# Score products of two attention stages: from three half-array passes per head to two full-array passes

## The chip, the cores and the metric

The kernel runs on one core of one Trainium2 chip. The metric is device time in microseconds, the median of several runs of the whole program. TensorE (PE in the rows) multiplies, VectorE (DVE) and ScalarE (ACT) do the elementwise work, SyncE (SP), ScalarE and GpSimd (POOL) issue the DMAs.

## The reference

Two blocks run one after the other on 512 tokens of 1024 features, all in float32. The first block has two layers and also carries 256 context tokens. Each layer computes a modulated RMS norm, one wide input projection, a gated convolution, neighbourhood attention (NA: 8 heads, a bias per head), window attention (WA: 8 query heads over 2 key heads, a window of 128 tokens on either side, a sink) and a gated sum of the three. What matters here is the window attention:

```python
def window_attention(q, k, v, k_ctx, v_ctx, sink):
    ...
        s_w = jnp.einsum('bqkgd,bskd->bkgqs', q_n, k_n).astype(jnp.float32) * scale
        s_w = jnp.where(valid, s_w, -jnp.inf)
        s_c = jnp.einsum('bqkgd,bnkd->bkgqn', q_n, k_ctx).astype(jnp.float32) * scale
        p = sink_softmax(jnp.concatenate([s_w, s_c], axis=-1), sink_b).astype(v.dtype)
```

The second block is a gated linear recurrence, a convolutional feed-forward layer, a sparse attention and another feed-forward layer. The sparse attention has 16 query heads over 4 key heads of 64 features and three branches: compressed keys, selected blocks (at 512 tokens all eight blocks are chosen, so this is causal attention) and a window of 512 (causal too). Both of the last two compute, per head,

```python
        s = jnp.einsum('bgrqd,bgkd->bgrqk', qc, kw, preferred_element_type=f32)
        s = s - sl * dist_w.astype(f32)
        p = masked_softmax(s, m_w)
```

## The kernel before

Float32 products are made exact by splitting each operand into two float32r parts, a high and a low one, and summing three products: high by high, high by low, low by high. Almost all products are of this kind, with 128 rows of the array in use: `mm_t` (L140 to L142, moving tiles of 512 or 256 columns) and `mm_n` (L151 to L153, 256 columns).

An attention head has 64 features, so a head's queries and keys take 64 rows. Two heads of a pair lie on rows 0 to 63 and 64 to 127, each head's high and low queries in two column ranges of the same rows. `scores` (L489) issues, for each of the three combinations of parts, one matmul per head of the unit, on the two halves of the rows in turn. NA has its own form of it at L516. In the sparse attention `scores` (L1457) does the same for a pair of heads, a query block and a branch.

The keys of WA (`Kw`) and of the sparse branches (`KS`) already lie on both halves of the rows, since the heads of a pair share a key head.

Work in WA comes in units. Per layer, two groups `u` of four heads, two pairs in each; a pair has the units (query block 0, both heads), (1, head 0), (1, head 1), (2, head 0), (2, head 1), (3, both heads), and in layer 0 two more for the context's queries. A unit's scores go to PSUM banks of the tag "s" (four of them), its softmax is done by DVE and ACT, and three units later its probabilities are transposed (`att_tr`, L582 and L585) and, at the end of a pair, multiplied with the values (`pv`, L609 and L630). `weave` mixes other products in as fill: the queries of the next group, gates, the input of the convolution and, in the last group, single taps of the convolution on DVE (L911).

The queries of WA are made by `wa_q`: product, RMS norm per head, rotation on DVE, four transposes, and then `to_T_nat` (L477 to L482) writes both parts, high by ACT and low by DVE, in natural token order. The context's queries go through `to_T` (L462 to L468). The transposes of the last token group are held back in `pend` until a later product has been issued.

The sparse attention handles two heads `f` at a time: `queries` makes the product, scales it on DVE into `qf`, splits it into `Q` (`split`, L199 and L200), and writes the distance bias `M`. Units are (branch, query block) in the order of `KORD`; a unit is closed two units later (transposes L1518, and after a branch's last unit the product with the values, L1526). The queries of the next two heads are mixed in as fill, by a budget of 0.32 of the TensorE time that each unit reports.

Engines execute their own instructions in order. The order is fixed when the program is built, by a scheduler that takes the program's order as priority and may pull later work forward when its inputs and a buffer are there. `wh`, `wl` (four buffers each) and `wr` (two) hold weights and are shared with `Q`, and `M`.

Of the kernel before, what the change touches and what calls it, by code (L numbers as in the profile page):

```python
# [19 lines left out]
P = 128  # L20
# [24 lines left out]
PTQ = (0, 0, 1, 2)                  # first query block that meets a key block's band  # L45
PT0 = (0, 2, 5, 8)                  # where its probabilities start
# [8 lines left out]
def weave(main, fill, ratio):  # L55
    """both in step: for each unit of tensor engine time of main, ratio units of fill; then the rest of fill"""
# [12 lines left out]
class K:  # L69
    """Pools and the pieces that both blocks use."""  # L70
# [22 lines left out]
    # ---- PSUM tiles: one bank each  # L93
# [15 lines left out]
    # ---- weights: a part is loaded and split exactly into two float32r tiles  # L109
# [5 lines left out]
    def load_w(self, src, kt, m, prio=50):  # L115
        """src [128, kt * m] -> per k tile the pair of parts [128, m]"""
# [28 lines left out]
    # ---- out[token, feature] += act[k, token] W[k, feature]  # L145
# [10 lines left out]
    # ---- 1/sqrt(v) for a small tile, from the bits and three Newton steps  # L156
# [46 lines left out]
# x tokens in the first block: column by column, the last 8 columns first  # L203
# [3 lines left out]
def nat(n, b, g=None):  # L207
    """pairs of views with axes (column, row): of n [p, 512] in natural order
    and of b, in block order, whole or its half g"""
# [6 lines left out]
def first_block(k):  # L216
# [24 lines left out]
    # ---- modulation: part 0 (shift and scale, in two halves of the features) and part 1 (gate)  # L241
    MOD, GS, GATE = {}, {}, {}

    def mod_pieces(l, part, h, pool, tag, bufs, psum=k.s_):
        """a product of 1024 columns for both streams, as background pieces"""
# [45 lines left out]
    for l in range(2):  # L291
# [15 lines left out]
        with tc.tile_pool(reuse_waits="tile", name=f"nrm{l}", bufs=2) as np_:  # L307
# [55 lines left out]
            if l == 0:  # L363
                # keys and values of the first heads: the first half of the sum runs while
                # the second half of the modulation comes in
# [46 lines left out]
        with tc.tile_pool(reuse_waits="tile", name=f"att{l}", bufs=2) as ap:  # L412
# [79 lines left out]
            def att_qk(un):  # L492
# [36 lines left out]
                if nb:  # L529
                    scores(heads, sb, Q, qi, K_, ki, qb * P, un["band"][0] * P, nb)  # L530
# [1183 lines left out]
```

## Time and profile before

| What | Value |
|---|---|
| Median of 3 runs | 2909.45 us (2908.74 to 2911.26) |
| Span of the profiled execution | 2907.6 us |
| Difference of the two | 1.85 us |
| PE busy | 2847.9 us, 98% |
| DVE busy | 1950.6 us, 67% |
| ACT busy | 1116.1 us, 38% |
| WA of layer 0, layer 1 (first to last score product) | 328 to 478 us, 1177 to 1279 us |
| Sparse attention | 2244 to 2450 us |

The profiled execution's own time is its span, 2907.6 us, and 1.85 us lie around it when it is set beside the median. Matmuls overlap one another, and their ends are modelled, so what a matmul costs is read from the distance between the starts of two matmuls that follow each other and not from its duration. A row of the timeline merges neighbours of one kind: it gives the start of the first, the time to the end of the last, and their number.

### The profile page before, as it was taken

What the parts mean: (1) busy time and instruction counts of PE and PEld (TensorE: products, weight loads), DVE (VectorE), ACT (ScalarE), POOL (GpSimd) and SP (SyncE); (2) the same over time, 40 slices, a digit from 0 to 9 for tenths busy, and PEclk for the clock granted to TensorE, in tenths of its full rate; (3) what the DMA queues carried; (4) which work ended last, traced back from release to release, by engine and by line L of the source; (5) the groups of instructions that cost most, each with busy time, mean ns of one, the idle gap of its engine ahead of it and who ended that gap; (6) DMA issues with size and microseconds to landing.
All of it is one profiled execution on the core that took longest, in us unless ns stands there. A gap on an engine that the chain in (4) does not pass through costs nothing.

```text
span 2907.6 us, 41432 instructions
## 1 busy us (share of the span) xinstructions
PE 2847.9 (98%) x15812; PEld 2317.3 (80%) x15812; DVE 1950.6 (67%) x4673; ACT 1116.1 (38%) x2218; POOL 0.7 (0%) x6
## 2 busy tenths in 40 slices
PE   6999999999999999999999999999999999999998
PEld 4887877788887888778888878888888666888886
DVE  5667789994544667999757866636543777663663
ACT  4444453122322444542334743222333666322221
POOL 0000000000000000000000000000000000000000
PEclk9999999999999999999999999999999999999999
DMA  6111011531224221112233232232242001223322
GB/s 222 65 63 50 31 37 52 159 110 59 67 75 158 90 73 62 44 57 91 100 106 104 95 101 96 89 107 98 90 133 98 23 16 51 95 91 98 102 89 78
DMA packets 79542, 248.68 MB, mean 86 GB/s; under 512 B 8944, under 2 KB 16496, under 8 KB 79344
## 3 DMA queue, kind: packets, MB, share of 16 engines
q1 hardware_dynamic: 75888, 238.69, 25.4%
q10 hardware_dynamic: 3456, 7.34, 0.8%
q8 instruction: 125, 2.05, 0.3%
q14 instruction: 73, 0.60, 0.1%
HBM read 239.71 MB, written 4.19 MB: 84 GB/s over the span
## 4 chain that ended last, share of the span: by engine, by line
PE 88%; DVE 4%; ACT 1%; DMA 1%; issue 1%; DVEq 0%; ACTq 0%
PE g L140 22%; PE g L142 21%; PE g L141 21%; PE g L151 3%; PE g L153 2%; PE g L152 2%; PE s L489 2%; PE s L1457 2%; PE g L1526 1%; PE t L1518 1%; PE o L609 1%; PE t L585 1%; PE t L582 1%; PE s L516 1%; DMA wada<-in_w_ada_dram 1%
## 5 line engine op out<-in xcount | busy, mean ns | idle before, releaser
L126 ACT CAST wh<-wr 128x1024 fp32r<-128x1024 f32 (+2 forms) x392 | 392.6, 1002 | 834.1 <-PE g L141 592.9
L140 PE MATMUL g<-Hh,wh 128*128 128x512 f32 x1736 | 690.6, 398 | 0.5 <-DVE Yb L1253 0.4
L141 PE MATMUL g<-Hl,wh 128*128 128x512 f32 x1736 | 682.0, 393 | 0.0
L142 PE MATMUL g<-Hh,wl 128*128 128x512 f32 x1736 | 681.7, 393 | 0.0
L127 DVE TENSOR_TENSOR wl<-wr,wh 128x1024 fp32r<-128x1024 f32 (+2 forms) x392 | 454.9, 1161 | 313.4 <-ACT wh L126 312.6
L140 PEld LDWEIGHTS g<-Hh,wh 128*128 128x128 f32 x1736 | 326.3, 188 | 77.8 <-issue 7.4
L142 PEld LDWEIGHTS g<-Hh,wl 128*128 128x128 f32 x1736 | 325.7, 188 | 72.8 <-issue 4.2
L141 PEld LDWEIGHTS g<-Hl,wh 128*128 128x128 f32 x1736 | 326.4, 188 | 66.2 <-issue 3.2
L151 PE MATMUL g<-wh,Hh 128*128 128x256 f32 x640 | 187.2, 293 | 1.6 <-ACT Hh L359 1.3
L911 DVE SCALAR_TENSOR_TENSOR cv<-apad,cv 128x499 f32<-128x499 f32 (+22 forms) x305 | 187.2, 665 | 0.6
L153 PE MATMUL g<-wh,Hl 128*128 128x256 f32 x640 | 183.2, 287 | 0.0
L152 PE MATMUL g<-wl,Hh 128*128 128x256 f32 x640 | 182.8, 286 | 0.0
L140 PE MATMUL g<-fh,wh 128*128 128x512 f32 x384 | 149.4, 389 | 0.0
L141 PE MATMUL g<-fl,wh 128*128 128x512 f32 x384 | 149.4, 389 | 0.0
L142 PE MATMUL g<-fh,wl 128*128 128x512 f32 x384 | 149.4, 389 | 0.0
L151 PEld LDWEIGHTS g<-wh,Hh 128*128 128x128 f32 x640 | 123.0, 192 | 9.2 <-issue 5.2
L153 PEld LDWEIGHTS g<-wh,Hl 128*128 128x128 f32 x640 | 122.4, 192 | 5.5 <-issue 4.1
L152 PEld LDWEIGHTS g<-wl,Hh 128*128 128x128 f32 x640 | 122.8, 192 | 1.3 <-issue 0.8
L1274 DVE TENSOR_TENSOR fxp<-g,nb 128x512 f32<-128x512 f32 x48 | 33.2, 692 | 127.9 <-PE g L142 127.9
L553 ACT ACTIVATE pr<-s,m 128x512 f32<-128x512 f32 (+1 forms) x128 | 80.8, 634 | 82.6 <-DVE m L551 61.1
L1166 DVE TENSOR_TENSOR Xs<-Xs,g 128x512 f32<-128x512 f32 x48 | 33.0, 688 | 113.6 <-PE g L142 113.5
L140 PE MATMUL g<-Ch,wh 128*128 128x256 f32 x352 | 101.2, 287 | 0.0
(403 smaller groups left out, 5240.1 us busy)
## 6 DMA issues: line engine op xcount, KB each, us to landing
wr<-in_ffn_w_in_dram SPq DMA_DIRECT2D x96, 512.0 KB, 3.4
wr<-in_w_in_t_dram SPq DMA_DIRECT2D x88, 512.0 KB, 3.4
wada<-in_w_ada_dram SPq DMA_DIRECT2D x48, 512.0 KB, 4.5
wr<-in_ffn_w_out_dram SPq DMA_DIRECT2D x64, 384.0 KB, 3.1
wr<-in_w_in_n_dram SPq DMA_DIRECT2D x32, 512.0 KB, 3.6
wr<-in_lru_w_in_dram SPq DMA_DIRECT2D x20, 512.0 KB, 3.4
wr<-in_w_o_dram SPq DMA_DIRECT2D x16, 512.0 KB, 3.5
bt<-in_nab_dram SPq DMA_DIRECT2D x48, 128.0 KB, 2.4
```

The source lines that it names most:

```text
L126: nc.scalar.copy(h[:, :n], r[:, :n])
L127: nc.vector.tensor_sub(lo[:, :n], r[:, :n], h[:, :n].bitcast(F32))
L140: mm(o, a, hi(k), start=k == 0, stop=False)
L141: mm(o, a, lo(k), start=False, stop=False)
L142: mm(o, b, hi(k), start=False, stop=k == KT - 1)
L151: mm(o, h, w[k][0], start=k == 0, stop=False)
L152: mm(o, h, w[k][1], start=False, stop=False)
L153: mm(o, lo(k)[:, t0:t0 + P], w[k][0], start=False, stop=k == KT - 1)
L489: nc.tensor.matmul(dst[i], Q[sl, a, qi, q0:q0 + P], K_[sl, b, ki, k0:k0 + kn], start=a + b == 0, stop=a == 1)
L553: AC.activation(pr, un["S"][i][:, :nb + 256], AF.Exp, bias=m[:, 2:3], accum_out=m[:, 3:4])
L911: V.scalar_tensor_tensor(d, src, wc, d, op0=ALU.mult, op1=ALU.add)
L1457: nc.tensor.matmul(S_[i][:, :nn], Q[sls[i], x, qb * P:(qb + 1) * P], KS[b][sls[i], y, g, :nn], start=x + y == 0, stop=x == 1)
```

## The change

The queries of a head of WA or of a sparse branch are laid out anew: its high part on one half of the 128 rows and its low part on the other, in one column range. A matmul over all 128 rows with the keys' high part (which lie on both halves) then gives high by high plus low by high in one go, and a second one with the keys' low part gives the rest (and low by low, which was left out before). So three matmuls of 64 rows per head become two of 128 rows. In WA, units with 256 band keys also do band and context in one matmul of 512 columns instead of two of 256. NA keeps its three passes.

[...] In WA the DMAs (`swap`) are issued on GpSimd's queue, once for all 512 tokens of a group and once for the context's queries; the temporary is `btall`, which held NA's biases before and holds early convolution taps later. In the sparse attention they are issued on SP's queue, and the temporary is a buffer of the tag "wl". Lines that only lose a comment are left out.

```diff
+            def to_T2(raw, dst, g, gain, tmp):
+                t = k.t_()
...
+                tv = t.rearrange("p (a n) -> p a n", a=2)
+                d4 = dst.rearrange("p (a i) n -> p a i n", i=2)
+                x = tmp.rearrange("p (a n) -> p a n", a=2)
+                c = slice(g * 256, g * 256 + 256)
+                for lo, h, l_ in ((0, d4[0:64, :, 0, c], x[0:64]), (64, x[64:128], d4[64:128, :, 1, c])):
+                    sl = slice(lo, lo + 64)
+                    AC.activation(h, tv[sl], AF.Identity, scale=gain[sl])
+                    V.scalar_tensor_tensor(l_, tv[sl], gain[sl], h.bitcast(F32), op0=ALU.mult, op1=ALU.subtract)
+                swap(d4, x, c)
+
+            def swap(d4, x, c):
+                nc.gpsimd.dma_start(out=d4[64:128, :, 0, c].bitcast(F32), in_=x[0:64].bitcast(F32))
+                nc.gpsimd.dma_start(out=d4[0:64, :, 1, c].bitcast(F32), in_=x[64:128].bitcast(F32))
+
+            def to_T2_nat(raw, dst, g, tmp):
...
+                for pr in range(2):
+                    tv = t[:, pr * 256:(pr + 1) * 256]
+                    for i, hi, lo in ((0, dst[:, 2 * pr, 0:S], tmp[:, pr]), (1, tmp[:, pr], dst[:, 2 * pr + 1, 0:S])):
+                        sl = slice(64 * i, 64 * i + 64)
+                        for (h, b), (l_, _) in zip(nat(hi[sl], tv[sl], g), nat(lo[sl], tv[sl], g)):
+                            AC.copy(h, b)
+                            V.tensor_sub(l_, b, h.bitcast(F32))
+                if g == 1:
+                    swap(dst.rearrange("p (a i) n -> p a i n", i=2), tmp, slice(0, S))
...
-            def scores(heads, dst, Q, qi, K_, ki, q0, k0, kn):
+            def scores(na, heads, dst, Q, qi, K_, ki, q0, k0, kn):
+                if not na:
+                    for i in heads:
+                        for b in range(2):
+                            kk = K_[:, b, ki, k0[0]:k0[0] + kn]
+                            if len(k0) > 1:
+                                kk = bass.AP(tensor=kk.tensor, offset=kk.offset, ap=[list(kk.ap[0]), [k0[1] - k0[0], 2], [1, kn]])
+                            nc.tensor.matmul(dst[i], Q[:, 2 * qi + i, q0:q0 + P], kk, start=b == 0, stop=b == 1)
+                    return
                 for a, b in ((0, 0), (0, 1), (1, 0)):
...
-                scores(heads, sc_, Q, qi, K_, ki, qb * P, 512, 256)
-                if nb:
-                    scores(heads, sb, Q, qi, K_, ki, qb * P, un["band"][0] * P, nb)
-                return len(heads) * 3 * (256 + nb) / 2400
+                if nb == 256:
+                    two = lambda v: v.rearrange("p (s n) -> p s n", s=2)
+                    scores(na, heads, {i: two(S_[i]) for i in heads}, Q, qi, K_, ki, qb * P, (un["band"][0] * P, S), 256)
...
+                return len(heads) * (3 if na else 2) * (256 + nb) / 2400
...
             def wa_q(u):
-                QW[u] = slot("qw", F32R).rearrange("p (s a n) -> p s a n", s=2, a=2)
+                QW[u] = slot("qw", F32R).rearrange("p (h n) -> p h n", h=4)
+                tmp = btall.bitcast(F32R).rearrange("p (a n) -> p a n", a=2)
...
-                        pend.append(lambda r=rope(raw, rq, g, 4, 1), g=g: to_T_nat(r, QW[u], g))
+                        pend.append(lambda r=rope(raw, rq, g, 4, 1), g=g: to_T2_nat(r, QW[u], g, tmp))
                     else:
-                        pend.append(lambda r=raw: to_T(r, QW[u], 2, qg[:, 1:2]))
+                        pend.append(lambda r=raw: to_T2(r, QW[u], 2, qg[:, 1:2],
+                                                        ap.tile([P, 512], F32R, tag="raw", name=k.nm("qx"), bufs=NRAW)))
...
-                Q = k.wp.tile([P, WMAX], F32R, tag="wh", name=k.nm("nQ"), bufs=4).rearrange("p (a n) -> p a n", a=2)
+                Q = k.wp.tile([P, WMAX], F32R, tag="wh", name=k.nm("nQ"), bufs=4).rearrange("p (i n) -> p i n", i=2)
+                qx = k.wp.tile([P, WMAX], F32R, tag="wl", name=k.nm("qx"), bufs=4)[:, :S]
                 st["Q"] = Q
-                k.split(Q[:, 0], Q[:, 1], qf)
+                k.split(Q[0:64, 0], qx[0:64], qf[0:64])
+                k.split(qx[64:128], Q[64:128, 1], qf[64:128])
+                nc.sync.dma_start(out=Q[64:128, 0].bitcast(F32), in_=qx[0:64].bitcast(F32))
+                nc.sync.dma_start(out=Q[0:64, 1].bitcast(F32), in_=qx[64:128].bitcast(F32))
...
-                for x, y in ((0, 0), (0, 1), (1, 0)):
-                    for i in range(2):
-                        nc.tensor.matmul(S_[i][:, :nn], Q[sls[i], x, qb * P:(qb + 1) * P], KS[b][sls[i], y, g, :nn],
-                                         start=x + y == 0, stop=x == 1)
-                return 6 * nn / 2400
+                for i in range(2):
+                    for y in range(2):
+                        nc.tensor.matmul(S_[i][:, :nn], Q[:, i, qb * P:(qb + 1) * P], KS[b][:, y, g, :nn],
+                                         start=y == 0, stop=y == 1)
+                return 4 * nn / 2400
```

## Rows read from the trace of the kernel before

**Rows 1.** Page, parts 1 and 4: busy time; the chain that ended last, by engine.
```profile
PE 2847.9 (98%) x15812; PEld 2317.3 (80%) x15812; DVE 1950.6 (67%) x4673; ACT 1116.1 (38%) x2218; POOL 0.7 (0%) x6
...
PE 88%; DVE 4%; ACT 1%; DMA 1%; issue 1%; DVEq 0%; ACTq 0%
```

**Rows 2.** Groups by line and form: xcount | busy us, mean ns | idle before.
```profile
L489 PE MATMUL s<-kw,qw 64*128 64x256 f32 x336 | 45.7, 304 | 0.4 <-ACT qw L481 0.2
...
L1457 PE MATMUL s<-KS,nQ 64*128 64x256 f32 x192 | 25.4, 326 | 1.4 <-ACT nQ L199 1.4
...
L489 PE MATMUL s<-kw,qw 64*128 64x384 f32 x96 | 23.8, 354 | 0.0
...
L1457 PE MATMUL s<-KS,nQ 64*128 64x512 f32 x96 | 20.7, 443 | 0.0
...
L1457 PE MATMUL s<-KS,nQ 64*128 64x384 f32 x96 | 16.6, 378 | 0.0
```

**Rows 3.** Timeline, all engines, 2251.0 to 2251.1: start, us, what.
```profile
2251.04 0.39 PE L1457 MATMUL s<-KS,nQ 64*128 64x256 f32 x2
```

**Rows 4.** Timeline of PE in WA, layer 1, around one unit of one head.
```profile
1239.36 0.40 PE L141 MATMUL g<-Hl,wh 128*128 128x512 f32 x1
1239.68 0.61 PE L489 MATMUL s<-kw,qw 64*128 64x256 f32 x3
1240.23 0.50 PE L142 MATMUL g<-Hh,wl 128*128 128x512 f32 x1
1240.57 0.40 PE L140 MATMUL g<-Hh,wh 128*128 128x512 f32 x1
```

**Rows 5.** Timeline of PE in WA, layer 0: full-array matmuls of 256 columns.
```profile
348.88 0.28 PE L152 MATMUL g<-wl,Ch 128*128 128x256 f32 x1
349.00 0.28 PE L153 MATMUL g<-wh,Cl 128*128 128x256 f32 x1
```

**Rows 6.** Timeline of PE in the sparse attention, around one paired unit.
```profile
2250.45 0.66 PE L1518 MATMUL t<-ident,pr 128*128 128x128 f32 x4
2251.04 0.63 PE L1457 MATMUL s<-KS,nQ 64*128 64x256 f32 x6
2251.73 0.63 PE L1518 MATMUL t<-ident,pr 128*128 128x128 f32 x4
```

**Rows 7.** Windows: WA of layer 0 (two), layer 1; then the sparse attention's sum.
```profile
328.00:408.00 80.00, 77.87 (x485) 56.78 (x484) 63.48 (x286) 42.22 (x132) 0.00 (x0) 1.00 0.07 24
408.00:500.00 92.00, 91.81 (x568) 71.90 (x568) 83.97 (x281) 43.77 (x132) 0.00 (x0) 1.00 0.11 35
1177.00:1285.00 108.00, 107.76 (x602) 75.74 (x601) 96.74 (x381) 62.10 (x184) 0.00 (x0) 1.00 0.12 40
...
sum 206.00, PE 204.32 PEld 134.08 DVE 164.27 ACT 147.57 POOL 0.00; mean PE 40.86 PEld 26.82 DVE 32.85 ACT 29.51 POOL 0.00
```

**Rows 8.** Windows: the convolution's taps beside the merge, layer 1.
```profile
1300.00:1380.00 80.00, 80.00 (x354) 66.24 (x353) 79.69 (x113) 21.81 (x29) 0.00 (x0) 1.00 0.28 93
```

**Rows 9.** Groups by line and form, DVE, 300 to 332: the queries' low parts.
```profile
L482 DVE TENSOR_TENSOR qw<-t,qw 128x256 fp32r<-128x256 f32 x2 | 1.2, 615 | 0.2 <-ACT qw L481 0.2
L482 DVE TENSOR_TENSOR qw<-t,qw 128x192 fp32r<-128x192 f32 x2 | 1.0, 506 | 0.2
...
L482 DVE TENSOR_TENSOR qw<-t,qw 128x64 fp32r<-128x64 f32 x2 | 0.6, 276 | 0.2
```

**Rows 10.** Groups by line and form in the sparse attention: the queries' split.
```profile
L200 DVE TENSOR_TENSOR nQ<-qf,nQ 128x512 fp32r<-128x512 f32 x8 | 5.5, 686 | 0.7 <-ACT nQ L199 0.7
```

**Rows 11.** DMA issues: KB each, median us from issue to landing.
```profile
bt<-in_nab_dram SPq DMA_DIRECT2D x48, 128.0 KB, 2.4
...
cD<-ct SPq DMA_DIRECT2D x4, 255.5 KB, 4.6
```

**Rows 12.** Timeline, 2290 to 2298: two heads' queries and the first product with them.
```profile
2291.73 0.64 ACT L199 CAST nQ<-qf 128x512 fp32r<-128x512 f32 x1
...
2293.32 0.39 PE L1457 MATMUL s<-KS,nQ 64*128 64x256 f32 x2
```

More of the change, by code (lines that the diff above doesn't have):

```diff
@@ L469, in to_T @@
                                            op0=ALU.mult, op1=ALU.subtract)
+            def to_T2(raw, dst, g, gain, tmp):
+                t = k.t_()
+                for pr in range(2):
+                    for j in range(2):
+                        nc.tensor.transpose(t[:, pr * 256 + j * P:pr * 256 + (j + 1) * P],
+                                            raw[:, j * 256 + pr * P:j * 256 + (pr + 1) * P], k.ident)
+                tv = t.rearrange("p (a n) -> p a n", a=2)
[11 more added lines that the diff above has]
+            def to_T2_nat(raw, dst, g, tmp):
+                t = k.t_()
+                rr = raw.rearrange("p (j a d) -> p j a d", j=2, a=2)
+                for pr in range(2):
+                    for j in range(2):
+                        nc.tensor.transpose(t[:, pr * 256 + j * P:pr * 256 + (j + 1) * P], rr[:, j, pr], k.ident)
+                for pr in range(2):
+                    tv = t[:, pr * 256:(pr + 1) * 256]
[6 more added lines that the diff above has]
+                    swap(dst.rearrange("p (a i) n -> p a i n", i=2), tmp, slice(0, S))
             def to_T_nat(raw, dst, g):
@@ L488, in scores @@
                         sl = slice(64 * i, 64 * i + 64)
-                        nc.tensor.matmul(dst[i], Q[sl, a, qi, q0:q0 + P], K_[sl, b, ki, k0:k0 + kn],
+                        nc.tensor.matmul(dst[i], Q[sl, a, qi, q0:q0 + P], K_[sl, b, ki, k0[0]:k0[0] + kn],
                                          start=a + b == 0, stop=a == 1)
@@ L527, in att_qk @@
                 un["sc"], un["sb"] = sc_, sb
-                scores(heads, sc_, Q, qi, K_, ki, qb * P, 512, 256)
-                if nb:
-                    scores(heads, sb, Q, qi, K_, ki, qb * P, un["band"][0] * P, nb)
-                return len(heads) * 3 * (256 + nb) / 2400
+                na = un["grp"]["na"]
+                if nb == 256:
+                    two = lambda v: v.rearrange("p (s n) -> p s n", s=2)
+                    scores(na, heads, {i: two(S_[i]) for i in heads}, Q, qi, K_, ki, qb * P, (un["band"][0] * P, S), 256)
+                else:
+                    scores(na, heads, sc_, Q, qi, K_, ki, qb * P, (S,), 256)
+                    if nb:
+                        scores(na, heads, sb, Q, qi, K_, ki, qb * P, (un["band"][0] * P,), nb)
+                return len(heads) * (3 if na else 2) * (256 + nb) / 2400
             nrm_ = [0]
@@ L1425, in nsa @@
             U = [k.bp.tile([P, 4, S], F32, tag=t, name=k.nm("nU")) for t in ("Ch", "Cl")]
-            sls = (slice(0, 64), slice(64, 128))
             def queries(f, st):
```

## Prediction

> **What bounds the kernel now.** I read the page first. PE is busy 98% of the span and makes up 88% of the chain that ended last, against 4% for DVE [rows 1]. A busy PE is not PE at its peak, so the next question is what a score product costs on PE. The groups by line and form give 432 WA matmuls and 384 sparse ones [rows 2]. The mean of one times the count is far above the group's busy time (304 ns by 336 is 102 us, against 45.7 us): they overlap. The timeline shows how: two matmuls of 64 rows, one of each head, fit into 0.39 us, hardly more than the 0.326 us of one [rows 2, 3]. So a pair on the two halves of the rows runs at the same time, and a unit of both heads pays three passes and not six. On column counts alone the change, with four full passes in place of three shared ones, loses.
>
> The distances between starts tell another story. Full-array matmuls of 512 columns follow each other at 80.00/354 = 0.226 us [rows 8], those of 256 columns at 0.12 us [rows 5]. Around a unit of one head in WA, L141 starts at 1239.36 and should hand over 0.226 us later; the three score products start 0.09 us after that, take 0.55 us to the next start, and the full-array matmul behind them needs 0.34 us to its successor, 0.11 more than it should [rows 4]. Together 0.75 us for what three dense passes of 256 columns would do in 0.36. In the sparse attention a paired unit takes 0.69 us from its start to that of the next transposes, for three shared passes of 0.12 [rows 6]. Going into matmuls of half the rows and coming back costs about 0.1 us each time, and the first pair's weights are not loaded under other work.
>
> The Trainium skill, "TensorEngine Tiling (Array Packing)", has both sides: its table of theoretical speedups gives up to twice the rate to products over 64 rows or fewer, which speaks against leaving them; its key properties say that changing the tiling mode drains the engine, which is what the 0.1 us look like. By the first alone the gain below would be about 3 us and not 69; by the second it stands.
>
> Last, the windows say who could stop PE from using the time: DVE is busy 147.5 of 172 us in WA of layer 0, 96.7 of 108 in layer 1, 164.3 of 206 in the sparse attention [rows 7].
>
> **The change part by part.**
>
> *Score products on PE.* I went through the timeline of PE run by run (a run is score products with nothing between them) and took from each the distance from the start before it to the start after it, less the dense distance of the product before, plus the excess of the full-array product after it. WA of layer 0: 47 runs, 43.7 us. Layer 1: 33 runs, 34.3 us. Sparse: 95 runs, 69.9 us without the one wait of 1.4 us [rows 2]. The new products are two thirds as many, each at the full-array distance (0.12 and 0.226 us; 0.173 for 384 columns, in between): WA (336 x 0.12 + 96 x 0.173) x 2/3 = 38.0 us, sparse (192 x 0.12 + 96 x 0.173 + 96 x 0.226) x 2/3 = 40.9 us [rows 2, 5, 8]. WA divides into 20.9 and 17.1 us. So PE is relieved of 22.8, 17.2 and 29.0 us, 69 in all. WA gains most for its size because most of its units are of one head: only 174 of 336 and 2 of 96 ran as pairs in my count, against 330 of 384 in the sparse attention.
>
> *What DVE lets through.* The low parts are now made in half-row instructions: a row's time goes by its columns, so two of 64 rows cost twice one of 128. Per group `u`, L482 ran 2 x 0.276 + 2 x 0.506 for the first token group and 2 x 0.615 for the second [rows 9], so DVE gets 2.8 us more; the context's queries in layer 0 some 0.75 more each. Inside the WA stretches that is 4.3 us (layer 0) and 2.8 us (layer 1); in the sparse attention 8 x 0.686 = 5.5 us [rows 10]. ACT's doubling lies beside this and has room (86 of 172 us busy in layer 0) [rows 7]. A stage of softmaxes was at most 91% full on DVE, one of taps 99.6% [rows 7, 8]; I take 96% as what DVE can reach, as the stage ahead is of both kinds. Then layer 0's stretch can shrink to (147.5 + 4.3)/0.96 = 158 us, a gain of 14; layer 1's to 99.5/0.96 = 103.7, a gain of 4; the sparse attention's to 169.8/0.96 = 177, which is just what PE needs, a gain of 29. Sum 47 of the 69. What DVE hands on late in WA, it hands to the merge, where PE is dense and DVE is 99.6% full [rows 8], so I give nothing back there.
>
> *The queries come later.* Before, the first product with new queries started at 2293.32, 0.95 us after ACT's high part was done at 2292.37 and ahead of the low part, which only the third pass needs [rows 12]. Now the first product needs both parts and two DMAs. The extra half-row instructions take about 0.69 on DVE. No row shows a DMA on GpSimd's queue, nor one of this size within SBUF on SP's; the nearest are 2.4 us for 128 KB from HBM and 4.6 us for 255.5 KB within SBUF [rows 11]. I take 3.5 us, nearer to neither. So queries are 3.1 to 5.3 us later, about 4.5 with what DVE has queued ahead.
> Sparse attention: the first two heads have nothing to hide it, +5 us (3.7 to 5.9). At the seven later ones PE has closes and fill of the next heads, but all softmaxes stand still meanwhile, and DVE has no slack to make that good; the smaller budget (4 passes reported and not 6) also ends the queries' product later in the unit order. I take half, 2.5 us each, +17.5 (0 to 41).
> WA: the group's first unit follows its queries at once at three places (layer 0 and 1, first group, and layer 1, second group); in layer 0 the second group's were long ready. The fill is larger there: +1.5 us each, +4.5 (0 to 16).
> The extra DVE work ahead of the first WA unit in each layer is under products of gates; half of 2 x 2.8 shows, +2.8 (0 to 5.6).
>
> *Sum.* -47 + 5 + 17.5 + 4.5 + 2.8 = -17 us. The profiled span is 2907.6, so 2890.4; with 1.85 us around it, 2892 us.
>
> What is at no cost: `btall` is free between NA's biases and the early taps, and the swaps read it before the taps begin; the merged 512-column product costs 0.226 where two of 256 cost 0.24.
>
> **Rivals.**
> 1. *Waits hidden.* The scheduler pulls enough fill forward at every head, and DVE keeps to 96%: only the first heads' 4 us remain, -43 us, 2866. For it: closes and fill at each change of heads, PE idle is rare now. Against: DVE at 96% and all softmaxes behind the queries.
> 2. *The queries' DMAs become the bound (slower).* At the seven changes of heads and three places in WA the wait is not covered: 5.9 + 41 + 16 + 5.6 = 68, less 47, +21 us, 2931. It decides when the uncovered wait passes about 4 us per head on average (47 less 5 and 7, over seven heads is 5; with the 0.2% bound 5.8). The place is the first L1457 product of each pair of heads. What would bring it about is SP's queue: a weight load waiting for its buffer ahead of the two DMAs.
> 3. *The switch is not what the tally says.* If the 0.1 us are not tied to the row halves and stay, only passes count: shared passes as they ran come to 82 us, the new to 79, so -3, and the queries' costs remain: +27, 2936; if these are hidden too, 2907. Against: the 0.09 and 0.11 us stand on either side of score products and not between full-array ones [rows 4, 5].
>
> **How the numbers follow.** A few tenths of a per cent is what separates runs, so 0.2%, 5.8 us, is what a measurement tells from none. My forecast (costs partly hidden, 2866 to 2903) has 0.58; rival 1 and better 0.14; costs nearly as large as the gain, 2904 to 2915, 0.12; rival 2 0.12; rival 3 0.04. Faster 0.72, same 0.12, slower 0.16. The range reaches from a little past rival 1 to the upper edge of no change: 2862 to 2914.
>
> **What would show it.** Right: no 64-row score products outside NA; L489 and L1457 products of 256 columns 0.12 us apart, and no 0.1 us on either side; sparse attention near 185 us and not 206; WA stretches shorter by 10 and 2 us; the merge unchanged. Wrong: PE idle before the first L1457 product of each pair of heads, put down to a DMA into nQ, of over 4 us; DVE below 80% in the sparse attention; the swaps in WA landing later than 5 us after issue. If DVE passes 96% in the sparse attention, the forecast is too high.

## The result, and the profile after

The changed kernel takes 2934.62 us (median of 4 runs, 2932.77 to 2936.0) against 2909.09 us of the kernel before on the same chip: 1.0088 times as long, 95% interval 1.0075 to 1.0101. It is slower by 25.5 us, where 17 us less were forecast. Its profiled span is 2932.4 us. In the changed kernel one part of each head's queries is written in place; the other goes to a temporary and from there by a DMA to the other half of the rows. No run writes it there without a DMA, so it is not shown that the transfer is needed. Line numbers of the changed kernel: L532 and L1516 are the score products of WA and of the sparse branches (before L489 and L1457), L1577 and L1585 the sparse attention's transposes and value products, L505/L506 WA's queries, L1486 `qf`, L1493 and L1494 the two DMAs of the queries.

Part 1 of the page after, which answers to [rows 1]:

```profile
PE 2830.4 (97%) x15476; PEld 2315.1 (79%) x15476; DVE 1970.0 (67%) x4707; ACT 1132.1 (39%) x2252; POOL 7.9 (0%) x18
```

PE is busy 17.5 us less and the end comes 25 us later, so PE stands still more. The windows of [rows 7], the same stretches in the kernel after (columns: stretch, its length, busy us of PE, its weight loads, DVE, ACT, POOL, the granted clock, DMA share, GB/s):

```profile
328.00:408.00 80.00, 67.01 (x390) 52.04 (x391) 69.23 (x292) 44.54 (x137) 3.65 (x6) 0.90 0.17 51
408.00:500.00 92.00, 89.77 (x530) 70.69 (x531) 81.99 (x286) 44.94 (x136) 1.18 (x2) 0.99 0.11 33
1177.00:1285.00 108.00, 98.07 (x510) 74.18 (x509) 93.28 (x359) 59.82 (x167) 2.34 (x4) 0.95 0.17 53
```

PE was busy 77.9 of the first 80 us and is now busy 67.0; in layer 1 it falls from 107.8 to 98.1 of 108, and the mean granted clock is 0.90 and 0.95 where it was 1.00.

Marks in the two traces show where the time went: the start of the merge of layer 0 (the product with `uah`), the last compression product of the keys ahead of the sparse attention, and the start of the sparse attention's output product. The second stretch holds WA of layer 1. The table of all runs stands with the experiments; the first two lines of it are 770.7, 1454.7, 222.2 and 460.0 us before, and 778.4, 1460.9, 233.1 and 460.0 us after. So WA of layer 0 gives 7.7 us, the stretch with WA of layer 1 6.2 us, the sparse attention 10.9 us, and nothing outside them moved.

A part of this is the clock. PE was busy 52.4 us at the granted clock 0.50 (1.2 of 2.4 GHz) in the whole execution after, against 18.6 us before. At the full clock the difference would have taken half the time, so by this estimate up to some 17 of the 25 us are matmuls at the lower clock; no run shows how much of that would come back. The stretches stand behind new waits of PE, as the last section shows, and where these waits come from is what the experiments ask.

The products did become what the change wanted. The timeline of PE in the sparse attention after, which answers to [rows 6] (start, us to the end of the last, engine, line, operation, count):

```profile
2322.40 0.39 PE L142 MATMUL g<-Hh,wl 128*128 128x512 f32 x1
2322.63 0.86 PE L1516 MATMUL s<-KS,nQ 128*128 128x384 f32 x4
2323.34 0.60 PE L1577 MATMUL t<-ident,pr 128*128 128x128 f32 x4
2323.69 0.72 PE L1516 MATMUL s<-KS,nQ 128*128 128x256 f32 x4
2324.25 0.60 PE L1577 MATMUL t<-ident,pr 128*128 128x128 f32 x4
```

A unit of 256 columns takes 0.56 us from its start to that of the transposes, against 0.69, and L142 hands over after 0.23 us, with no switch to see. The loss is at the change of heads. All engines from the scaling of two heads' queries to their first score product, after (the last column is the idle time before and what ended it):

```profile
2279.44 0.68 DVE L1486 SCALAR_TENSOR_TENSOR qf<-g,nb 128x512 f32<-128x512 f32 x1
...
2280.50 0.62 ACT L199 CAST nQ<-qf 64x512 fp32r<-64x512 f32 x1
...
2281.16 0.68 DVE L200 TENSOR_TENSOR qx<-qf,nQ 64x512 fp32r<-64x512 f32 x1 [0.26 <-ACT nQ L199]
2281.33 1.03 ACT L126 CAST wh<-wr 128x1024 fp32r<-128x1024 f32 x1
...
2282.39 0.62 ACT L199 CAST qx<-qf 64x512 fp32r<-64x512 f32 x1
2282.42 0.19 PEld L140 LDWEIGHTS g<-Hh,wh 128*128 128x128 f32 x1 [1.61 <-ACT wh L126]
...
2282.97 1.22 DVE L127 TENSOR_TENSOR wl<-wr,wh 128x1024 fp32r<-128x1024 f32 x1
2283.03 0.46 SPq L1494 DMA_DIRECT2D nQ<-qx  x1
...
2284.22 0.69 DVE L200 TENSOR_TENSOR nQ<-qf,qx 64x512 fp32r<-64x512 f32 x1
2284.24 0.29 PEld L142 LDWEIGHTS g<-Hh,wl 128*128 128x128 f32 x1 [1.52 <-DVE wl L127]
...
2286.86 0.80 PE L1516 MATMUL s<-KS,nQ 128*128 128x256 f32 x2
...
2287.81 0.43 DVE L1545 CUSTOM_DVE_ANT_0 s<-s,M 128x256 f32<-128x256 f32 x1 [2.90 <-PE s L1516]
```

From the end of `qf` (2280.12) to the first score are 6.74 us here, where the granted clock was 0.50 from 2282.9 to 2289.8, and 5.35 at most heads, against 1.71 before (`qf` ended at 2291.61, the score is in [rows 12]). The half-row instructions stand on ACT and DVE between the two instructions that split the next weights, so PE waits for those too (L140 for ACT's L126, L142 for DVE's L127), and the softmaxes on DVE start 2.9 us after DVE ran dry. A half-row instruction takes as long as a whole one: 0.68 us on DVE here for 64 rows, 0.686 for 128 in [rows 10]. The next change of heads, PE alone and then windows of 2 us across it (columns as above):

```profile
2311.61 1.07 PE L1585 MATMUL g<-PT,VS 128*64 128x512 f32 x2
2313.26 0.50 PE L140 MATMUL g<-Hh,wh 128*128 128x512 f32 x1 [0.58 <-ACT wh L126]
...
2315.08 0.50 PE L142 MATMUL g<-Hh,wl 128*128 128x512 f32 x1 [0.64 <-DVE wl L127]
2315.51 1.07 PE L1585 MATMUL g<-PT,VS 128*64 128x512 f32 x4
2316.51 0.50 PE L1516 MATMUL s<-KS,nQ 128*128 128x256 f32 x2
2316.95 0.86 PE L1585 MATMUL g<-PT,VS 128*64 128x384 f32 x4
...
2318.17 0.86 PE L1585 MATMUL g<-PT,VS 128*64 128x256 f32 x6
```

```profile
2312.00:2314.00 2.00, 1.41 (x4) 0.30 (x2) 1.90 (x6) 1.95 (x4) 0.00 (x0) 1.00 0.05 13
2314.00:2316.00 2.00, 1.33 (x7) 0.58 (x7) 1.94 (x3) 1.18 (x3) 0.00 (x0) 1.00 0.51 118
2316.00:2318.00 2.00, 2.00 (x12) 0.76 (x8) 0.69 (x3) 0.31 (x1) 0.00 (x0) 1.00 0.80 256
```

The sixteen value products L1585, elsewhere one run of 2.39 us, are stretched over 7.4 us, with some 1.4 us of other products between them. So about 3.6 us are lost, while first ACT and DVE are full and then, from 2316, nearly empty. PE's own wait for the DMAs hardly shows here: the list of PE's waits gives 0.5 us for the whole sparse attention. In WA it gives 4.4 us, at the first units of a group: 0.3 us in layer 0, 3.2 and 0.9 us in layer 1. The pitch from head to head is 27.4 us against 26.55 before.

### The profile page after: what moved, and what is told of

Its sections match the earlier page's. It is cut to its first block, busy times and chain, and to the rows that moved or that the text cites. A ratio compares the mean times of both kernels' runs of the same rounds, so it can differ in the third digit from the quotient of the medians.

```text
span 2932.4 us, 40984 instructions
## 1 busy us (share of the span) xinstructions
PE 2830.4 (97%) x15476; PEld 2315.1 (79%) x15476; DVE 1970.0 (67%) x4707; ACT 1132.1 (39%) x2252; POOL 7.9 (0%) x18
## 4 chain that ended last, share of the span: by engine, by line
PE 53%; issue 3%; DVE 2%; ACT 1%; DMA 1%; DVEq 0%; ACTq 0%; POOLq 0%
PE g L142 15%; PE g L140 15%; PE g L141 15%; PE s L1516 1%; PE g L1585 1%; PE t L1577 1%; DVE wl L127 1%; PE s L1442 0%; PE g L153 0%; PE g L151 0%; PE g L152 0%; PE s L532 0%; ACT PT L1580 0%; PE g L1563 0%; DVE W L1292 0%
## 5 line engine op out<-in xcount | busy, mean ns | idle before, releaser
L126 ACT CAST wh<-wr 128x1024 fp32r<-128x1024 f32 (+2 forms) x392 | 392.2, 1001 | 820.2 <-PE g L141 569.2
L140 PE MATMUL g<-Hh,wh 128*128 128x512 f32 x1736 | 690.8, 398 | 8.1 <-ACT wh L126 6.7
L142 PE MATMUL g<-Hh,wl 128*128 128x512 f32 x1736 | 683.4, 394 | 4.6 <-DVE wl L127 4.6
L127 DVE TENSOR_TENSOR wl<-wr,wh 128x1024 fp32r<-128x1024 f32 (+2 forms) x392 | 455.1, 1162 | 313.9 <-ACT wh L126 312.8
L140 PEld LDWEIGHTS g<-Hh,wh 128*128 128x128 f32 x1736 | 326.8, 188 | 87.5 <-ACT wh L126 12.5
L142 PEld LDWEIGHTS g<-Hh,wl 128*128 128x128 f32 x1736 | 326.8, 188 | 74.5 <-DVE wl L127 7.0
L966 DVE SCALAR_TENSOR_TENSOR cv<-apad,cv 128x507 f32<-128x507 f32 (+24 forms) x305 | 187.7, 667 | 0.6
L140 PE MATMUL g<-fh,wh 128*128 128x512 f32 x384 | 149.6, 390 | 0.0
L142 PE MATMUL g<-fh,wl 128*128 128x512 f32 x384 | 149.6, 390 | 0.0
L1022 ACT ACTIVATE th<-g 128x512 f32<-128x512 f32 x72 | 37.5, 521 | 166.8 <-PE g L142 146.4
```

The source lines that it names most:

```text
L126: nc.scalar.copy(h[:, :n], r[:, :n])
L127: nc.vector.tensor_sub(lo[:, :n], r[:, :n], h[:, :n].bitcast(F32))
L140: mm(o, a, hi(k), start=k == 0, stop=False)
L142: mm(o, b, hi(k), start=False, stop=k == KT - 1)
L966: V.scalar_tensor_tensor(d, src, wc, d, op0=ALU.mult, op1=ALU.add)
L1022: lambda o, n0, n1: AC.activation(th[:, n0:n1], o, AF.Tanh, scale=0.5)))
```

## Experiments

Theories. **A**: the queries are ready too late, and the fill that should cover it is not there. **B**: the smaller reported time of a unit thins the fill. **C**: the full products gain nothing. The rival to A in the later runs is that the added work on ACT and DVE costs the time wherever it stands.

All runs, with the marks of their profiled executions in us: start of the merge of layer 0; from there to the end of the keys' compression; the sparse attention up to its output product; the span. The ratio is to the kernel before on the same chip. A mark comes from one execution: runs with the same WA code differ by up to 5.3 us at the first mark (e6, 776.3, and e18, 781.6) and by 3.5 us in the second stretch (e15 and e17).

| Run | Median | Ratio (95%) | Merge l0 | WA l1 stretch | Sparse | Span |
|---|---|---|---|---|---|---|
| before | 2909.09 | 1 | 770.7 | 1454.7 | 222.2 | 2907.6 |
| after | 2934.62 | 1.0088 (1.0075, 1.0101) | 778.4 | 1460.9 | 233.1 | 2932.4 |
| e1_budget | 2931.19 | 1.0072 (1.0057, 1.0087) | 771.8 | 1460.9 | 234.3 | 2926.8 |
| e2_products | 2885.97 | 0.9916 (0.9901, 0.9931) | 768.2 | 1449.0 | 207.6 | 2885.2 |
| e3_prep | 2949.94 | 1.0135 (1.0115, 1.0155) | 781.8 | 1467.5 | 235.1 | 2945.3 |
| e4_products_budget | 2875.88 | 0.9884 (0.9865, 0.9903) | 758.6 | 1449.5 | 203.3 | 2872.7 |
| e5_sparse_only | 2920.55 | 1.0036 (1.0023, 1.0050) | 770.4 | 1454.9 | 232.7 | 2918.8 |
| e6_wa_only | 2923.88 | 1.0049 (1.0033, 1.0066) | 776.3 | 1460.6 | 222.1 | 2919.8 |
| e7_halfrows | 2908.08 | 0.9990 (0.9981, 1.0000) | 774.4 | 1457.0 | 215.6 | 2907.1 |
| e8_dma_only | 2905.70 | 0.9983 (0.9973, 0.9992) | 766.9 | 1458.6 | 218.5 | 2903.1 |
| e9_early | 2916.29 | 1.0022 (1.0012, 1.0031) | 776.3 | 1454.5 | 228.6 | 2920.8 |
| e10_before_early | 2910.83 | 1.0006 (0.9996, 1.0015) | 770.5 | 1455.8 | 223.9 | 2910.1 |
| e11_onelow_early | 2901.83 | 0.9972 (0.9961, 0.9982) | 760.4 | 1453.1 | 226.3 | 2898.7 |
| e12_onelow | 2920.46 | 1.0034 (1.0022, 1.0047) | 768.7 | 1458.8 | 232.9 | 2920.8 |
| e13_even_onelow | 2893.37 | 0.9944 (0.9929, 0.9958) | 761.7 | 1451.5 | 216.7 | 2891.9 |
| e14_even_full | 2904.87 | 0.9983 (0.9973, 0.9992) | 775.3 | 1456.1 | 217.3 | 2907.8 |
| e15_even_onelow_lead3 | 2895.76 | 0.9951 (0.9936, 0.9966) | 760.7 | 1451.2 | 218.9 | 2889.7 |
| e16_before_even | 2906.63 | 0.9991 (0.9981, 1.0000) | 768.8 | 1455.7 | 219.0 | 2903.3 |
| e17_even_onelow_qx | 2888.53 | 0.9929 (0.9912, 0.9946) | 762.4 | 1454.7 | 208.2 | 2885.8 |
| e18_after_qx | 2928.72 | 1.0066 (1.0051, 1.0081) | 781.6 | 1461.1 | 224.7 | 2926.5 |

**Products, preparation and reported times apart.** e1 reports the old times. e2 and e4 write the queries as before (so the full products multiply parts that don't belong together); e3 keeps the new preparation and DMAs, and issues the old 64-row products (which then also read the wrong parts).

```diff
-                return len(heads) * (3 if na else 2) * (256 + nb) / 2400   # e1, e3, e4
+                return len(heads) * 3 * (256 + nb) / 2400
-                return 4 * nn / 2400
+                return 6 * nn / 2400
-                k.split(Q[0:64, 0], qx[0:64], qf[0:64])                    # e2, e4; in WA to_T, to_T_nat again
...
+                k.split(Q[:, 0], Q[:, 1], qf)
-                        nc.tensor.matmul(S_[i][:, :nn], Q[:, i, qb * P:(qb + 1) * P], KS[b][:, y, g, :nn],
...
+                        nc.tensor.matmul(S_[i][:, :nn], Q[sl, x, qb * P:(qb + 1) * P], KS[b][sl, y, g, :nn],   # e3; WA too
```

> The changed kernel, but each unit reports the TensorE time of three passes again, so that the fill is mixed in at the old pace; nothing else differs. Theory A (the queries are ready too late: half-row instructions, then a DMA, and TensorE has nothing that can stand in): the pace of the fill hardly matters, 2928 to 2940 us. Theory B (the smaller reported time thins the fill among the units, so TensorE runs out of fill while softmaxes are awaited): 10 to 20 us come back, 2915 to 2925 us.

> The full-array products alone: queries are prepared as before the change (no half-row instructions, no DMA), and the new products read that layout, so that the scores are not those of the reference. The reported times are those of the changed kernel. Theory A: the products' gain is there and undisturbed, 2862 to 2885 us. Theory B: the thin fill still costs 10 to 20 us, 2885 to 2905 us. Theory C (the full-array products gain nothing, the loss is theirs): 2909 us or more.

> The preparation alone: half-row instructions and DMAs as in the changed kernel, but three passes of 64 rows as before, with their old reported times; the scores are not those of the reference. Theory A: the price of the late queries stands alone, 2945 to 2970 us. Theory B: close to before, 2909 to 2920 us. Theory C: close to before too.

> The full-array products alone (queries prepared as before the change, so that the scores are not those of the reference), with the old reported times. Theory A: within 6 us of the products alone with the new reported times, 2862 to 2885 us. Theory B: 10 to 20 us faster than with the new reported times.

C falls: the products alone save 34 us (2910.22 on that chip less 2875.88), by the marks 12.1, 5.2 and 18.9. The preparation alone costs 40 us (e3). B is a small part: 10 us between e2 and e4, 3.4 us between the changed kernel and e1. Beside the full products the preparation costs e1 less e4, 55 us by the medians and 13.2, 11.4 and 31.0 us by the marks. That is 15 us more than beside the old products.

**One stage at a time.** Each run is the changed kernel with the other stage as before.

```diff
-                k.split(Q[0:64, 0], qx[0:64], qf[0:64])          # e6: queries, scores and reported time as before
...
+                k.split(Q[:, 0], Q[:, 1], qf)
-                        pend.append(lambda r=rope(raw, rq, g, 4, 1), g=g: to_T2_nat(r, QW[u], g, tmp))   # e5: WA as before
+                        pend.append(lambda r=rope(raw, rq, g, 4, 1), g=g: to_T_nat(r, old, g))
```

> The change in the sparse attention alone; WA (its queries, products and reported times) is as before. If each stage pays for itself alone, the stage marks of the two first traces give it: the sparse stage is 10.9 us longer in the changed kernel, so about 2920 us. Theory A (queries ready too late) also wants the stage itself at about 233 us and PE's distance from the queries' scaling to the first score at about 6 to 7 us. If what WA does shifts the scheduler's later choices, the time is off 2920 by more than 4 us.

> The change in WA alone; the sparse attention is as before. By the stage marks 7.7 us (layer 0) and 6.4 us (layer 1) more than before: about 2923 us, and the sparse stage at 222 us. A result under 2911 would say that WA's part of the loss came from the sparse change.

Both as the marks said, 2920.6 and 2923.9 us: the stages add up, and each can be read from its own column.

**Half-row instructions or transfers.**

```diff
-                k.split(Q[0:64, 0], qx[0:64], qf[0:64])          # e7, no transfers; WA likewise
-                k.split(qx[64:128], Q[64:128, 1], qf[64:128])
-                nc.sync.dma_start(out=Q[64:128, 0].bitcast(F32), in_=qx[0:64].bitcast(F32))
-                nc.sync.dma_start(out=Q[0:64, 1].bitcast(F32), in_=qx[64:128].bitcast(F32))
+                k.split(Q[0:64, 0], Q[0:64, 1], qf[0:64])
+                k.split(Q[64:128, 0], Q[64:128, 1], qf[64:128])
...
+                k.split(Q[:, 0], qx, qf)                         # e8, full rows, transfers kept; WA likewise
+                nc.sync.dma_start(out=Q[64:128, 1].bitcast(F32), in_=qx[0:64].bitcast(F32))
+                nc.sync.dma_start(out=Q[0:64, 1].bitcast(F32), in_=qx[64:128].bitcast(F32))
```

> The full products with reported times as before, and queries written in half-row instructions on ACT and DVE, but each part on its own rows and with no transfer: a product then multiplies parts that don't belong together, so the scores are not the reference's, and the work on every engine except the transfers is that of the changed kernel. Between the full products with the old preparation (2876) and the changed kernel with the old reported times (2931) lie 55 us. Theory A1 (the doubled instructions on ACT and DVE, in series, make the queries late): 2910 to 2925. Theory A2 (the wait for the transfers makes them late): 2880 to 2890.

> The full products with reported times as before, queries written by as many instructions as in the kernel before, and the low part then transferred as in the changed kernel, but to rows where it doesn't belong, so the scores are not the reference's. In the sparse attention only the second head's products wait for the transfers. A1: 2880 to 2895. A2: 2915 to 2930. If this and the run with half-row instructions each add little to 2876, the two delays only hurt together, beyond what the fill covers.

Neither A1 nor A2 alone: 32 and 30 us over e4, each more than half of the 55. (e8 also takes the buffer of `wl` that the last two runs are about; e7 doesn't.) In the sparse attention 12.3 and 15.2 of 31.0 us; in layer 0 the instructions weigh more (15.8 against 8.3), in layer 1 about the same (7.5 and 9.1).

**The same work earlier, and lighter work.** e9 and e10 move the queries forward in the changed kernel and in the one before; e11 and e12 write the low part in one instruction on DVE, with and without the move.

```diff
-                    due += 0.32 * c                              # e9, e10, e11
+                    due += 0.6 * c
-            run(wa_kv(), w_gates(range(G0, G1)), wa_q(0))
...
+            run(wa_kv(), wa_q(0), w_gates(range(G0, G0 + 1)))
+            flush()
+            run(w_gates(range(G0 + 1, G1)))
...
-            last = pend[0]
-            while last in pend:
-                next(q1)
-                k.split(Q[0:64, 0], qx[0:64], qf[0:64])          # e11, e12; WA likewise
-                k.split(qx[64:128], Q[64:128, 1], qf[64:128])
+                k.split(Q[:, 0], qx, qf)
+                AC.copy(Q[64:128, 1], qf[64:128])
```

> The changed kernel with the old reported times (2931), and the queries made earlier: in the sparse attention the budget of the next heads' queries is 0.6 of the reported time and not 0.32, in WA the first group's queries stand ahead of the two gate products and not behind them. Nothing else is changed, and the work on every engine is the same. Theory A (late queries): the sparse stage falls from 234 to about 210 us, WA of layer 0 ends at about 762 us and not 772, the total is 2890 to 2900. Rival (the added work on DVE and ACT costs the time wherever it stands): 2925 to 2932.

> Control: the kernel before with the same two moves of the queries. If moving them helps only because the new queries are late, it stays within 5 us of 2910. If the old kernel gains as much as the changed one, earlier queries are a gain of their own and say nothing about the change.

> As the run before the control (queries early, old reported times), but with fewer instructions: DVE writes the low part of both heads in one instruction of 128 rows, ACT the high part likewise and the second head's high part once more on 64 rows, and the two transfers move the low part alone. The scores are the reference's. DVE's doubling is gone, a DMA is left. Theory A: 2880 to 2892, faster than both kernels. If only DVE's work counted, it would already come to about 2905 without the moves (next run).

> The same preparation with one low-part instruction, without the moves: queries as late as the transfers make them. By the run with transfers alone (2906) about 2908, with 2905 to 2915 as the span.

The control stays where it was. e9 gains 15 us by the medians, half of what A asked for. By the marks of its profiled execution, one of its longer ones (2911 to 2923), the WA stretch of layer 1 gets 6.4 us back and the sparse attention 5.7, while layer 0 loses 4.5. e12 misses its 2908 by 12 us: with ACT's extra copy the lighter preparation alone gives back 3.1 us in layer 0, 2.1 in layer 1 and 1.4 in the sparse attention. Both together do more (e11: 11.4, 7.8 and 8.0 us against e1), though e11 too stays 10 us short of its 2880 to 2892. Layer 0 wants the lighter work as well as the earlier place. The sparse attention had a new wait, which the timeline of PE in e9 shows (scores are L1515 there, value products L1584):

```profile
2289.61 0.42 PE L1515 MATMUL s<-KS,nQ 128*128 128x384 f32 x1
2292.43 1.53 PE L1515 MATMUL s<-KS,nQ 128*128 128x256 f32 x4 [2.39 <-ACT pr L1546]
2293.89 4.54 PE L1584 MATMUL g<-PT,VS 128*64 128x512 f32 x16
```

At 0.6 the next queries' product is used up in the first half of a head, and in the second half PE waits 2.4 us for a softmax, six times.

**Early, and fill everywhere.** One generator makes all queries, so the fill goes on across heads, with a lead (e13, e14, e16: 1.7 us; e15: 3.0). e13 and e15 have e11's preparation, e14 that of the changed kernel, e16 is the kernel before. These lines are against e11, e9 and e10.

```diff
+            fill = chain(*(queries(f, sts[f]) for f in range(1, 8)))
+            due = 1.7
+            while due > 0:
+                due -= next(fill, 1e9)
...
-                    due += 0.6 * c
+                    due += 0.305 * c
-                run(fill)
+                while f < 7 and "M" not in sts[f + 1]:
+                    due -= next(fill, 1e9)
```

> The lighter preparation with WA's queries early (2902), and in the sparse attention the queries as one continuous fill over all heads, at 0.305 of the reported time with a lead of 1.7 us, so that the next heads' are ready a quarter of a head early and fill is left everywhere. If the late queries cost the time: the sparse stage falls from 226 to 205 to 212 us, the total to 2880 to 2890. If the added work on ACT and DVE costs it: 222 to 226 us, 2897 to 2903.

> The same continuous fill with the preparation of the changed kernel (half-row instructions), WA's queries early. Late queries: the sparse stage falls from 229 to 208 to 216 us, the total from 2916 to about 2900. Added work: 2912 to 2917.

> As the first of these with a lead of 3.0 us instead of 1.7: if lateness is what is left, another few us less; if 1.7 covers it, the same within 3 us.

> Control: the kernel before with the same continuous fill, a lead of 1.7 us and WA's queries early. Its queries were in time, so within 5 us of 2910.

The sparse attention falls to 216.7 us (e13) and 217.3 us (e14), a little above what A asked for (212 and 216 at most): once the fill is even, it makes no difference whether half-row instructions or whole ones write the queries. That speaks for A in this stage, with 17 of the 31 us back; the rival would have kept e14 near 229. The queries are not early even so: in e14 a pair's first score starts 0.1 us after the first transfer has landed (2298.1 after 2298.0). What changed is that PE has fill up to there. The longer lead adds nothing. The control gains 3.4 us, so a little of it is the fill's own. In layer 0 the preparation does make a difference: e14 is 13.6 us behind e13 at the mark, and 11.5 us by the medians (e14's profiled execution was its longest). The first group's queries land within 1.2 us of each other there, so this speaks for the rival, but it doesn't decide: the second group's land up to 9 us later in e14 (the last at 409.8, against 401.3). Windows of e13, then of e14, in WA of layer 0 (columns as above):

```profile
370.00:390.00 20.00, 18.16 (x93) 11.04 (x93) 15.70 (x62) 9.10 (x30) 0.00 (x0) 0.91 0.17 54
```

```profile
370.00:390.00 20.00, 16.25 (x60) 8.66 (x61) 17.05 (x67) 9.26 (x30) 0.00 (x0) 0.74 0.10 30
```

DVE does 1.3 us more in this stretch and PE gets a third fewer matmuls done, part of them at the lower clock. From 340 us to the merge PE is busy 21.9 us at the granted clock 0.50 in e14 and 6.8 us in e13; half of the difference, 7.5 us, is more than half of the 13.6.

**The buffer.** What was left at each head were PE's waits for the split of the next weights. The temporary `qx` took one of the four buffers of `wl`; now it lies in the output tile of the same heads.

```diff
-                qx = k.wp.tile([P, WMAX], F32R, tag="wl", name=k.nm("qx"), bufs=4)[:, :S]
+                qx = U[f // 4][:, f % 4].bitcast(F32R)
```

> The version at 2893 with the queries' temporary outside the weights' buffers. If the buffer taken from the weights makes their split late: PE's waits for it (7.5 us in the stage) go, the sparse stage comes to 208 to 212 us, the total to 2884 to 2889. If not, 2892 to 2895 and the waits stay.

> The changed kernel with the temporary outside the weights' buffers, nothing else. In its trace PE waits 6.3 us in the stage for the weights' split. If the buffer is a cause of its own: 2926 to 2930 and a sparse stage of 225 to 229 us. If the split is late only because the queries' half-row instructions stand in front of it on ACT and DVE: 2933 to 2936.

The buffer is a cause of its own: 8.5 us less in the sparse attention with even fill, 8.4 us in the changed kernel. The medians fall by less, 4.8 and 5.9 us, since the WA marks of these two runs lie 0.2 to 3.2 us later, with WA code that is the same. PE's waits in the sparse attention (engine, line, for what; us, times, longest), of the changed kernel, then with the buffer moved (e18):

```profile
PE g L140 <- ACT wh L126: 6.7, 7, 2.4
PE g L142 <- DVE wl L127: 4.6, 7, 1.0
```

```profile
PE g L140 <- ACT wh L126: 6.2, 7, 2.4
PE g L142 <- DVE wl L127: 0.5, 1, 0.5
```

The wait for DVE's low part is gone, the one for ACT's high part stays. (PE waits 11.3 us for the split in the whole stage; the 6.3 us of the expectation are those from 2300 on.) e17 is the fastest version that computes what the reference does: 2888.5 us, 0.7% less than the kernel before.

## Why the prediction was wrong, point by point

*Where the miss lies.* The sum missed by 42 us. The largest part is the preparation in WA (24.6 us by the marks against 7.3), then the gain (35 against 47), the preparation in the sparse attention (31.0 against 22.5) and the smaller reported times (5.6, no term). The step that failed most is the one that set the extra work of ACT and DVE in WA at 2.8 us.

*The late queries.* "I take half, 2.5 us each, +17.5" held in size and not in mechanism. The delay was sized well: 3.6 us more from `qf` to the first score, against 3.1 to 5.3. e4's pitch from head to head is 24.0 us and the changed kernel's 27.4, so 3.4 us per head were lost; 0.8 of them go with the buffer alone (e18's pitch is 26.6), and 2.6 are left. (e18 has the new reported times and e4 the old, which make 1.2 us in this stage, after against e1.) That this comes so near to 2.5 is partly luck, since the cover that was to take the other half was not there. The "closes" are transposes and value products of the last softmaxes, and these waited for ACT too; the other fill, the next queries' product, waited for its weights. With larger losses at the first and the last change of heads the stage comes to 31 us (e1 less e4) against 22.5, and the buffer's 8.4 us are about the difference.

*WA.* "+1.5 each, +4.5" and "half of 2 x 2.8 shows, +2.8" came to 7.3; the runs give 24.6 (13.2 and 11.4). Each is too small by its own run: over e4 the transfers alone cost 17.4 us in the two WA stretches (e8), though PE itself waits only 4.4 us for them in the changed kernel, and the half-row instructions alone cost 23.3 (e7), where 2.8 was forecast. With the second falls "ACT's doubling lies beside this and has room": from 340 to 480 us PE is busy 126.6 us, where it was 138.5 before, and its waits of over 1 us there are for softmaxes and copies on ACT and for DVE. The timeline of ACT and DVE after, in WA of layer 0:

```profile
370.60 0.27 ACT L505 CAST qw<-t 64x64 fp32r<-64x64 f32 x1 [6.26 <-PE t L499]
...
370.89 0.27 DVE L506 TENSOR_TENSOR bt<-t,qw 64x64 fp32r<-64x64 f32 x1
...
371.74 0.48 ACT L505 CAST qw<-t 64x192 fp32r<-64x192 f32 x1
...
372.38 0.49 DVE L506 TENSOR_TENSOR bt<-t,qw 64x192 fp32r<-64x192 f32 x1
372.91 0.27 ACT L505 CAST bt<-t 64x64 fp32r<-64x64 f32 x1 [0.70 <-DVE bt L506]
```

Each low part waits for its high part, and the next high part stands behind that low part (0.70 us at 372.91), so both doublings lie in one chain. That the work itself counts in layer 0, and not only its place, is likely by e13 and e14 and not shown, as said there. Why one such microsecond costs PE several is settled in part: the waits are followed by stretches at half the clock, 7.5 us of PE's time in layer 0 and 4.7 in layer 1 by the windows at the end.

*Not in the sum.* The buffer that `qx` takes from the weights (8.4 us), and the smaller reported times (5.6 us by the spans, 3.4 by the medians), which the prediction named without a term, and for the sparse attention. By the marks they cost 6.6 us in layer 0 and nothing in the sparse attention; 6.6 is little above the scatter of that mark. The clock has no term either.

*The gain.* 69 us of relief and 47 let through were forecast; e4 gained 35. Run by run as in the prediction, e4's new products take 26.8, 20.7 and 52.3 us where 20.9, 17.1 and 40.9 were forecast, so the relief is 48 and not 69: a run of score products still pays about 0.13 us over the dense distance (21 us over 163 runs). So a part of the 0.1 us around [rows 4, 6] was not the row halves' doing, and rival 3 was right by a third. The drain that the Trainium skill ("TensorEngine Tiling (Array Packing)", key properties) describes agrees with the larger part, the relief of 48 us; no run here takes a drain apart from the rest of that relief. In WA 12.1 and 5.2 us of the relief show, close to the 14 and 4 that were forecast as DVE's limit, but e4 lacks the extra work on DVE that the forecast counted, so this doesn't confirm the limit. In the sparse attention the relief of 17.6 us showed in full (18.9).

*Sum by spans.* -35 for the products (e4 less before), +54 for the preparation (e1 less e4) and +6 for the reported times (after less e1) make the +25. Rival 2 gave 2931 and named late queries as its mechanism. That it came so near is partly luck: it took a gain of 47 and a cost of 68, where 35 and 60 were measured. Its trigger, a weight load ahead of the DMAs on SP's queue, is not in the trace: L1494 is issued as soon as its source is written. The sign to look for was wrong as well: no wait of over 4 us is put down to a DMA into nQ. The delay is spread over waits for ACT and DVE. "DVE below 80% in the sparse attention" did show (173.3 of 233 us, 74%) but tells nothing: between the same marks it was 166.3 of 222 us, 75%, before. The signs for "right" didn't fit the sum either: sparse attention 21 us shorter and WA 10 and 2 are 33 us, twice the 17 of the sum. The landings (3.9 us for 256 KB on GpSimd's queue, 2.2 for 128 KB on SP's) lie on both sides of the 3.5 us that were taken, and the merge (91.7 us, as before) was as forecast.

## What to carry to other kernels

Where an operand is prepared just in time, a longer preparation costs its delay once per use unless the fill at that very place is independent of the engines that do the preparing; list what stands in the queues there before calling any of it covered. Price a new layout by its preparation in series (who reads the same tile, whose buffer the temporary takes), and measure products and preparation apart: here -34 and +40 us. Look at the granted clock around each new wait before pricing it by its length. Issuing an operand's work early helps only if the fill that made it early is still there later: spread it with a lead, not with a higher rate.

## What the runs showed of the hardware

After the idle 2.39 us in e9 the clock fell. Windows of e9 across the rows of its timeline above:

```profile
2290.00:2292.00 2.00, 0.03 (x1) 0.00 (x0) 1.94 (x4) 1.98 (x4) 0.00 (x0) 1.00 0.15 35
2292.00:2294.00 2.00, 1.57 (x6) 1.12 (x8) 1.91 (x10) 2.00 (x9) 0.00 (x0) 0.55 0.41 96
2294.00:2296.00 2.00, 2.00 (x6) 0.66 (x8) 2.00 (x10) 1.50 (x4) 0.00 (x0) 0.50 0.00 0
2296.00:2298.00 2.00, 2.00 (x11) 0.93 (x8) 0.98 (x1) 0.00 (x0) 0.00 (x0) 0.50 0.11 12
```

The granted clock is 0.50 (1.2 of 2.4 GHz) for some 6 us, and the sixteen value products take 4.54 us instead of 2.39. So the wait cost nearly twice its length.

The lower mean clocks of the WA windows after are of this kind. These are the stretches at 0.50 in the changed kernel, three in WA of layer 0 and two in WA of layer 1, where the kernel before had 1.00 throughout [rows 7] (columns as above):

```profile
364.63:368.04 3.41, 3.41 (x13) 2.17 (x11) 2.85 (x7) 0.00 (x0) 0.00 (x0) 0.50 0.32 105
378.29:385.12 6.83, 5.78 (x17) 2.95 (x15) 4.86 (x19) 4.74 (x15) 0.00 (x0) 0.50 0.25 78
402.18:409.01 6.83, 5.80 (x16) 2.52 (x18) 4.46 (x19) 2.78 (x9) 1.17 (x2) 0.50 0.47 154
1197.48:1200.89 3.41, 3.41 (x11) 2.78 (x11) 3.38 (x16) 0.82 (x3) 0.00 (x0) 0.50 0.51 154
1217.96:1224.79 6.83, 5.97 (x18) 3.43 (x18) 6.13 (x29) 3.31 (x13) 0.00 (x0) 0.50 0.07 15
```

Each begins at or soon after the end of waits of PE: 2.5 us up to 363.5, 1.5 and 1.2 us up to 376.2 and 377.9, 2.3 us up to 402.3, 2.8 us up to 1196.1, 1.7 us up to 1216.3. PE is busy 15.0 us in the first three and 9.4 us in the other two; half of it, 7.5 and 4.7 us, is what the lower clock took by this estimate, against 7.7 and 6.2 us that the two stretches lost.
